# Ten of sixteen RWKV queries made beside the fronts and sent through DRAM, where four were kept on chip, and inversions that trace their products some rounds later

## The chip, the core and the metric

The kernel runs on one core of a Trainium2 chip. The core has five engines that run side by side, each through its own instructions in a fixed order: TensorE (PE) for matmuls, VectorE (DVE) and ScalarE (ACT) for elementwise work, GpSimd (POOL), and SyncE (SP), which here only issues DMA transfers; POOL issues some as well. An engine waits on semaphores for what another engine or a transfer has made. The metric is the device time of one execution in microseconds (us).

## The reference

One inference step of a two-layer encoder, D_MODEL = 2048, for 256 prompt tokens and 32 sample tokens (288 columns together). Layer 0 mixes with an mLSTM and an RG-LRU, layer 1 with RWKV-7 time mixing of 32 heads of 64; behind each mixer stands a squared-ReLU MLP. The change lies in layer 1:

```python
r = xr @ p['c_w_r'][li]
k = xk @ p['c_w_k'][li]
v = xv @ p['c_w_v'][li]
...
def step(S, inp):
    r_t, k_t, v_t, kk_t, a_t, w_t = inp
    sa = jnp.einsum('bhvk,bhk->bhv', S, -kk_t)
    S = S * w_t[:, :, None, :] + sa[..., None] * (kk_t * a_t)[:, :, None, :] + v_t[..., None] * k_t[:, :, None, :]
    return S, jnp.einsum('bhvk,bhk->bhv', S, r_t)
...
out = ((y + bonus) * g) @ p['c_w_o'][li]
```

`r` is the query that reads the state. The kernel works in chunks of 64 tokens, so for each head and chunk a triangular 64x64 matrix has to be inverted.

## The kernel before, in words

Heads are taken two at a time: 16 pairs of 128 rows. Dense products are made in three matmuls each (high and low part of the weights and of the activations), so the query of one pair is 16 tiles, 48 matmuls of 288 columns. Weights come in slabs of 8 tiles (512 KB, tile `raw`, three buffers); ACT makes the high part `whi` and DVE the low part `wlo`.

Two stages matter here.

**The fronts.** `run` advances generators by rounds, one step of each in a round, and a scheduler then orders the instructions. Three streams run: `front(p)` for each pair makes its decay and keys and stores them (`big`) and the matrix `nm` (`n`) in DRAM; `inverse16(q)` for each two pairs loads the 16x16 diagonal blocks (`nb`), inverts them on POOL in 15 steps of `tmp` and `tb`, and stores them (`t<-tb`); after some rounds (`for _ in range(5)`) `inverse(p, nm)` loads them as `tq`, and after some more (`range(3)`) traces the products on PE that make the inverse of 64x64, which is stored for later (`t<-tts`). The third stream makes `v` for pairs 2 to 15 (PE reads `hC`, `lC`), stored in DRAM, and then the queries of the first RPRE = 4 pairs in `r_proj` (PE reads `hD`, `lD`). These stay on chip in the dictionary RP. STEP and REST say after how many tiles a product of `r_proj` lets how many rounds pass.

**wkv.** `beside` advances `wkv(p)` of up to WIDTH = 4 pairs, a new one every GAP = 11 rounds, in the order in which it is written (no scheduler here). After each step of a pair it adds RATE divided by the number of pairs to an account, and for each SIZE = 4 in it advances the generator `feed` by four tiles. `feed` makes the remaining queries (`ps<-hD`, `ps<-lD`), then the first half of the output projection (`ps<-hB`, weights `in_wo`), which waits for the eighth pair's result. While RP holds RPC queries, `feed` yields and does nothing: the tiles of that turn are not made up for. `wkv(p)` takes its query out of RP in its fourth step; there DVE multiplies it into `ak` (`ak<-r,ak`) and POOL into `bk`. What `feed` has left after the last pair runs at the end.

A period of eleven rounds holds for one pair: loads on SP (`ak`, `bk`, `T`, `sv`, `v`), transposes (`pm<-cst,bk`, `pm<-cst,v`), products by chunk (`pm<-ak,bk`, `pm<-bm,T`), the chain of states through four prompt chunks and one sample chunk (`pm<-sv,ak`, `pm<-sv,tk`, `py`), the head norm with an inverse square root on DVE (`st<-st`), the gate (`ps<-hg`) and the result (`yc`, split into `hB`, `lB`).

Of the kernel before, what the change touches and what calls it, by code (L numbers as in the profile page):

```python
# [7 lines left out]
F32 = mybir.dt.float32  # L8
# [8 lines left out]
N = NP + NS  # L17
# [24 lines left out]
def stream_step(ctx: ExitStack, tc: tile.TileContext, I, O):  # L42
    nc = tc.nc
    V, A, G, PE, SP = nc.vector, nc.scalar, nc.gpsimd, nc.tensor, nc.sync

    def pool(name, bufs=1, side=None, **kw):
        st = ExitStack()
        if side is not None:
            kw['side'] = side
        p = st.enter_context(tc.tile_pool(name=name, bufs=bufs, reuse_waits="tile", **kw))  # L50
        return st, p
# [25 lines left out]
    def tt(out, a, b, op, eng=None):  # L77
        (eng or V).tensor_tensor(out=out, in0=a, in1=b, op=op)  # L78
# [21 lines left out]
    def copy(out, a):  # L100
        act(out, a, AF.Copy)

    def mm(out, lhsT, rhs, start=True, stop=True):
        PE.matmul(out, lhsT, rhs, start=start, stop=stop, skip_group_check=True)  # L104
# [106 lines left out]
    def dense_g(srcs, xs, m=128, step=4, rest=1):  # L211

        yield from hold()
        ps = psum.tile([128, 512], F32, name="ps", bufs=NPS)
        n = len(xs)
        for s, src in enumerate(srcs):
            kt = min(KS, n - s * KS)
            wh, wl = slab(src, kt, m)
            for k in range(kt):
                g = s * KS + k  # L220
                mm3(ps[:m, :N], (wh[:, k, :], wl[:, k, :]), xs[g], g == 0, g == n - 1)
                if g % step == step - 1:
                    for _ in range(rest):
                        yield
        free()
        return ps[:m, :N]
# [28 lines left out]
    def pm():  # L255
        return psum.tile([128, 512], F32, name="pm", tag="m", bufs=NPM)
# [545 lines left out]
    st_hid, hid = pool("hid", side="right")  # L802
# [185 lines left out]
    st_1, t1 = pool("t1")  # L988
# [4 lines left out]
    def scr(name, shape):  # L993
        return tc.dram_tile(shape, F32, name=name)
# [35 lines left out]

    RP = {}

    def r_proj(ps_):
        for p in ps_:
            while len(RP) == RPC:
                yield
            pr = yield from dense_g([I['wr'][p, s] for s in range(2)], xr, step=STEP, rest=REST)
            r = hid.tile([128, N], F32, name="r", tag="wa", bufs=4)
            copy(r, pr)
            RP[p] = r  # L1040
            yield

    NMB = 7
    GAPF = 6
    lastf = [-99]
    IE = G
    RPC, RPRE, GAP = 4, 4, 11
    WIDTH, RATE, SIZE, EXTRA = 4, 1.8, 4, 0.4
    NG = 1
    ended = set()  # L1050
    STEP, REST = 8, 6
    NM = {}
    done = set()
    def front(p):
# [64 lines left out]
    def flat(x):  # L1119
        return x.rearrange("p c t -> p (c t)")  # L1120

    def inverse16(q):

        while 2 * q + 1 not in NM:
            yield
        yield
        nb = t1.tile([80, 16, 16], F32, name="nb", bufs=1)
        G.dma_start(nb, bass.AP(tensor=SN[q].tensor, offset=SN[q].offset, ap=[[BS, 80], [C, 16], [1, 16]]))
        tb = t1.tile([80, 16, 16], F32, name="tb", bufs=2)
        SP.dma_start(tb, I['eye'])  # L1130
        for s in range(15):
            w, n = 15 - s, s + 1
            tmp = t1.tile([80, 64], F32, name="tmp", bufs=2)
            tv = tmp[:, :w * n].rearrange("p (a b) -> p a b", b=n)
            tt(tv, nb[:, s, s + 1:].unsqueeze(2).to_broadcast([80, w, n]),
               tb[:, s, :n].unsqueeze(1).to_broadcast([80, w, n]), OP.mult, eng=IE)
            tt(tb[:, s + 1:, :n], tb[:, s + 1:, :n], tv, OP.add, eng=IE)
            if s % 2:
                yield
        for i in range(2):  # L1140
            dst = bass.AP(tensor=S16[q].tensor, offset=S16[q].offset + i * (16 * 32 + 16),
                          ap=[[1024, 40], [32, 16], [1, 16]])
            G.dma_start(dst, tb[i:80:2])
        for _ in range(5):
            yield
        on = [inverse(2 * q, NM[2 * q]), inverse(2 * q + 1, NM[2 * q + 1])]
        while on:
            for g in list(on):
                try:
                    next(g)  # L1150
                except StopIteration:
                    on.remove(g)
            yield

    def inverse(p, nm):


        def f2(name):
            return t1.tile([128, NC, 32], F32, name=name, tag="f2", bufs=7)

        tq = f2("tq")
        G.dma_start(tq, S16[p // 2][p % 2].rearrange("c p t -> p c t"))

        def blocks(f):
            pz = pm()[:, :160].rearrange("p (c t) -> p c t", t=32)
            for c in range(NC):
                f(pz, c)
            return pz

        def quad(f):  # L1170
            def g(pz, c):
                for q in range(4):
                    r = slice(32 * q, 32 * q + 32)
                    l, x = f(r, 32 * (q % 2), c)
                    mm(pz[r, c, :], l, x)
            return blocks(g)

        for _ in range(3):
            yield
        xq = f2("xq")  # L1180
        V.transpose(flat(xq), flat(tq))
        pz = quad(lambda r, o, c: (nm[r, c, o:o + 32], tq[r, c, :]))
        yield
        zz = f2("zz")
        tt(zz, pz, mblk[:, None, :].to_broadcast([128, NC, 32]), OP.mult)
        yield
        pz = quad(lambda r, o, c: (xq[r, c, :], zz[r, c, :]))
        yield
        t32 = f2("t32")
        tt(t32, tq, pz, OP.add)  # L1190
        x32 = f2("x32")
        V.transpose(flat(x32), flat(t32))

        los = [slice(64 * h, 64 * h + 32) for h in range(2)]
        his = [slice(64 * h + 32, 64 * h + 64) for h in range(2)]

        def off(pz, c):
            for lo, hi in zip(los, his):
                mm(pz[hi, c, :], nm[lo, c, 32:64], t32[lo, c, :])

        yield
        pz = blocks(off)
        yield
        z2 = f2("z2")
        for hi in his:
            copy(z2[hi], pz[hi])

        def off2(pz, c):
            for hi in his:
                mm(pz[hi, c, :], x32[hi, c, :], z2[hi, c, :])  # L1210

        yield
        pz = blocks(off2)
        yield
        tt_ = tts[p % 2]
        for lo, hi in zip(los, his):
            copy(tt_[lo, :, 0], t32[lo])
            copy(tt_[hi, :, 1], t32[hi])
            copy(tt_[hi, :, 0], pz[hi])
        yield  # L1220
        SP.dma_start(ST[p], tt_)
        done.add(p)
# [63 lines left out]
    def ahead():  # L1286
        yield next(other)

    run(stream([front(p) for p in range(PAIRS)], 2), stream([inverse16(q) for q in range(PAIRS // 2)], 2),
        stream([v_proj(range(VPRE, PAIRS)), r_proj(range(RPRE)), ahead()], 1))  # L1290

    st_1.close()
# [7 lines left out]
    def f3(name, w=W, bufs=3):  # L1300
        return t2.tile([128, W], F32, name=name, bufs=bufs)[:, :w]
# [34 lines left out]
    def wkv(p):  # L1336
# [16 lines left out]
        pcs = bk[:, 2 * W + N:]  # L1353
        vf = f3("v", W, 4)
        DQ.dma_start(vf, SV[p])
        yield
        yield

        def tok(x, out):

            x = x.rearrange("p c t -> p (c t)")
            pz = pm()[:, :384].rearrange("p (a h t) -> p a h t", a=3, h=2)
            for j in range(3):
                w = 128 if j < 2 else 64
                PE.transpose(pz[:w, j].rearrange("p h t -> p (h t)"), x[:, 128 * j:128 * j + w], ident)  # L1365
            yield
            for i in range(2):
                for h in range(2):
                    copy(out(h)[:, i::2], pz[HH[i], :3 - i, h])
# [10 lines left out]

        bm = t2.tile([128, 2, NC, C], F32, name="bm", bufs=2)
        yield from tok(b_, lambda h: bm[HH[h], 0])
        while p not in RP:
            yield
        r = RP.pop(p)
        for h in range(2):
            R = flat(ak[HH[h], h, 1])[:, :N]
            tt(R, r[HH[h]], R, OP.mult)
# [120 lines left out]
    with tc.manual_schedule():  # L1509
        beside([wkv(p) for p in range(PAIRS)], WIDTH, GAP, other, RATE, SIZE)  # L1510
# [124 lines left out]
def _build(nc, arrays):  # L1635
    ins = {n: nc.dram_tensor(f"in_{n}", a.shape, F32, kind="ExternalInput").ap() for n, a in arrays.items()}
    outs = {n: nc.dram_tensor(f"out_{n}", s, F32, kind="ExternalOutput").ap() for n, s in _OUT.items()}
    with tile.TileContext(nc, schedule_with_timeline_sim=True) as tc:
        stream_step(tc, ins, outs)
# [13 lines left out]
```

## Time and profile before

| | us |
|---|---|
| median of three runs | 3341.88 (3338.5 to 3342.61) |
| the profiled execution | 3340.57 |
| its span, from first to last instruction | 3338.4 |
| PE busy | 3217.9 (96%) |
| DVE busy | 2120.1 (64%) |
| ACT busy | 1628.0 (49%) |
| POOL busy | 551.3 (17%) |

The profile is of one execution. Its page gives busy times by engine, the span in 40 slices, and the granted clock of PE (PEclk, 1.00 is full speed); views of the trace give the same for any stretch, the waits of an engine with what ended them, and the instructions in order of time. Times of a view count from the start of the span. Busy time of PE includes time in which its pipeline is only being filled; a share near 100% says that it waited for nothing, not that it worked at its peak. The page's line of PE by slices has nines nearly throughout, except in the slices of the fronts and some before them, in which also the clock falls; the fronts lie at about 1858 to 2100 us, wkv at about 2100 to 2432.

### The profile page before, as it was taken

The page shows a single profiled execution, that of the slowest core. Times are in us where ns is not written, and L with a number is a line of the kernel's source. Part 1 is how long each engine was busy: PE and PEld are TensorE (multiplying, and loading weights), DVE is VectorE, ACT ScalarE, POOL GpSimd, SP SyncE. Part 2 cuts the span into 40 slices and gives each one's busy share as a digit, 9 for nine tenths or more (in the row PEclk, how much of TensorE's full clock was granted, in tenths as well). Part 3 has the DMA queues.
Part 4 walks back from the last instruction along what each step waited for, and adds up shares of the span by engine and source line. Part 5 has one row for each costly group of instructions (what it writes and reads, how often), then busy time and mean ns, then how long its engine had stood idle before and what let it go on. Part 6 is the DMA issues. An engine that isn't in the chain of part 4 may idle for free.

```text
span 3338.4 us, 66879 instructions
## 1 busy us (share of the span) xinstructions
PE 3217.9 (96%) x26763; PEld 3120.9 (93%) x26763; DVE 2120.1 (64%) x3838; ACT 1628.0 (49%) x3070; POOL 551.3 (17%) x899
## 2 busy tenths in 40 slices
PE   9999999999999999999889888999989999999997
PEld 8999999999999999999878877788889999999997
DVE  6777777755655545456588664677777455454565
ACT  4444444444634435345465554676646344353443
POOL 0101111111000000001488256111240000000013
PEclk9999999999999999999999978999999999999998
DMA  6444444455554554555444765444454555555553
GB/s 209 149 154 156 151 156 147 146 180 180 164 167 165 165 165 165 164 165 160 162 125 138 235 201 162 149 137 136 152 171 161 167 165 165 164 164 165 165 164 123
DMA packets 195081, 540.60 MB, mean 162 GB/s; under 512 B 39179, under 2 KB 74251, under 8 KB 194771
## 3 DMA queue, kind: packets, MB, share of 16 engines
q1 hardware_dynamic: 190322, 526.95, 48.8%
q0 software_dynamic: 4448, 9.39, 1.2%
q8 instruction: 210, 3.44, 0.4%
q14 instruction: 101, 0.82, 0.1%
HBM read 500.81 MB, written 35.41 MB: 161 GB/s over the span
## 4 chain that ended last, share of the span: by engine, by line
PE 36%; POOL 4%; DVE 3%; DMA 3%; issue 2%; ACT 2%; SPq 0%; ACTq 0%; POOLq 0%; DVEq 0%
PE ps L104 32%; PE pm L104 3%; POOL tb L78 1%; POOL xx L78 1%; DVE wlo L78 1%; DVE x L78 1%; POOL tmp L78 1%; DMA t<-tb 1%; DMA nb<-n 1%; PE pm L1365 1%; PE py L104 0%; DMA tq<-t 0%; DMA v<-v 0%; ACT whi L98 0%; POOL xx L81 0%
## 5 line engine op out<-in xcount | busy, mean ns | idle before, releaser
L78 DVE TENSOR_TENSOR wlo<-raw,whi 128x1024 fp32r<-128x1024 f32 (+1 forms) x1018 | 1102.0, 1090 | 842.2 <-ACT whi L98 836.0
L98 ACT ACTIVATE whi<-raw 128x1024 fp32r<-128x1024 f32 (+1 forms) x1018 | 942.5, 936 | 1297.1 <-PE ps L104 1137.3
L104 PE MATMUL ps<-hB,whi 128*128 128x290 f32 (+1 forms) x3792 | 1133.9, 299 | 9.2 <-DVE x L78 2.8
L104 PE MATMUL ps<-hB,wlo 128*128 128x290 f32 (+1 forms) x3792 | 1131.3, 298 | 4.4 <-DVE wlo L78 4.4
L104 PE MATMUL ps<-lB,whi 128*128 128x290 f32 (+1 forms) x3792 | 1126.4, 297 | 4.9 <-DVE lB L78 4.9
L104 PEld LDWEIGHTS ps<-hB,whi 128*128 128x128 f32 x3792 | 718.8, 190 | 16.2 <-issue 5.1
L104 PEld LDWEIGHTS ps<-lB,whi 128*128 128x128 f32 x3792 | 719.9, 190 | 10.7 <-DVE lB L78 6.3
L104 PEld LDWEIGHTS ps<-hB,wlo 128*128 128x128 f32 x3792 | 717.3, 189 | 7.2 <-DVE wlo L78 6.0
L104 PE MATMUL ps<-hD,wlo 128*128 128x288 f32 (+1 forms) x1584 | 469.4, 297 | 6.6 <-DVE wlo L78 6.6
L104 PE MATMUL ps<-hD,whi 128*128 128x288 f32 (+1 forms) x1584 | 475.0, 300 | 0.3 <-ACT whi L98 0.3
L104 PE MATMUL ps<-lD,whi 128*128 128x288 f32 (+1 forms) x1584 | 468.9, 296 | 3.2 <-POOL lD L78 1.8
L104 PE MATMUL ps<-hC,whi 128*128 128x288 f32 (+1 forms) x1552 | 462.5, 298 | 5.4 <-ACT v L98 4.5
L104 PE MATMUL ps<-hC,wlo 128*128 128x288 f32 (+1 forms) x1552 | 460.2, 297 | 0.0
L104 PE MATMUL ps<-lC,whi 128*128 128x288 f32 (+1 forms) x1552 | 459.1, 296 | 0.0
L104 PEld LDWEIGHTS ps<-hD,wlo 128*128 128x128 f32 (+1 forms) x1584 | 300.3, 190 | 8.1 <-DVE wlo L78 7.9
L104 PEld LDWEIGHTS ps<-lD,whi 128*128 128x128 f32 (+1 forms) x1584 | 300.5, 190 | 4.1 <-POOL lD L78 2.0
L104 PEld LDWEIGHTS ps<-hD,whi 128*128 128x128 f32 (+1 forms) x1584 | 299.5, 189 | 4.5 <-issue 1.9
L104 PEld LDWEIGHTS ps<-hC,whi 128*128 128x128 f32 (+1 forms) x1552 | 293.5, 189 | 6.8 <-ACT v L98 5.6
L104 PEld LDWEIGHTS ps<-lC,whi 128*128 128x128 f32 (+1 forms) x1552 | 295.3, 190 | 0.3
L104 PEld LDWEIGHTS ps<-hC,wlo 128*128 128x128 f32 (+1 forms) x1552 | 294.4, 190 | 0.4
L78 POOL TENSOR_TENSOR acc<-x,x 128x288 f32<-128x288 f32 x8 | 8.6, 1079 | 1515.4 <-DVE x L78 1511.5
L78 DVE TENSOR_TENSOR x<-x,ps 128x288 f32<-128x288 f32 x96 | 43.6, 454 | 101.3 <-PE ps L104 100.6
(355 smaller groups left out, 3345.9 us busy)
## 6 DMA issues: line engine op xcount, KB each, us to landing
raw<-in_w SPq DMA_DIRECT2D x512, 512.0 KB, 3.4
raw<-in_win SPq DMA_DIRECT2D x160, 512.0 KB, 3.3
raw<-in_wout SPq DMA_DIRECT2D x64, 512.0 KB, 3.3
raw<-in_wk SPq DMA_DIRECT2D x32, 512.0 KB, 3.4
raw<-in_wv SPq DMA_DIRECT2D x32, 512.0 KB, 4.1
raw<-in_wr SPq DMA_DIRECT2D x32, 512.0 KB, 4.0
raw<-in_wo SPq DMA_DIRECT2D x32, 512.0 KB, 3.4
big<-big SPq DMA_DIRECT2D x16, 786.5 KB, 4.8
```

What stands on the lines that cost most here:

```text
L78: (eng or V).tensor_tensor(out=out, in0=a, in1=b, op=op)
L98: return A.activation(out, a, f, **kw)
L104: PE.matmul(out, lhsT, rhs, start=start, stop=stop, skip_group_check=True)
L1365: PE.transpose(pz[:w, j].rearrange("p h t -> p (h t)"), x[:, 128 * j:128 * j + w], ident)
```

## The change

`r_proj` now makes the queries of pairs 0 to 9 (RPRE = 10), each in a tile of its own pool, and stores it in DRAM (`SR[p]`) instead of keeping it; `wkv(p)` loads it into the tile that `feed` uses for its queries, as the last of its loads. `feed` has six queries left instead of twelve, and RP may hold two (RPC) instead of four. RATE goes from 1.8 to 1.3; STEP and REST from 8 and 6 to 4 and 2. The inversions let eight rounds pass instead of five before `inverse`, and six instead of three before its products.

```diff
--- before.py
+++ after.py
@@ -1030,25 +1030,26 @@
 
     RP = {}
 
+    SR = {}
+
     def r_proj(ps_):
         for p in ps_:
-            while len(RP) == RPC:
-                yield
             pr = yield from dense_g([I['wr'][p, s] for s in range(2)], xr, step=STEP, rest=REST)
-            r = hid.tile([128, N], F32, name="r", tag="wa", bufs=4)
+            r = t1.tile([128, N], F32, name="r", bufs=2)
             copy(r, pr)
-            RP[p] = r
+            SR[p] = scr(f"r{p}", [128, N])
+            SP.dma_start(SR[p], r)
             yield
 
     NMB = 7
     GAPF = 6
     lastf = [-99]
     IE = G
-    RPC, RPRE, GAP = 4, 4, 11
-    WIDTH, RATE, SIZE, EXTRA = 4, 1.8, 4, 0.4
+    RPC, RPRE, GAP = 2, 10, 11
+    WIDTH, RATE, SIZE, EXTRA = 4, 1.3, 4, 0.4
     NG = 1
     ended = set()
-    STEP, REST = 8, 6
+    STEP, REST = 4, 2
     NM = {}
     done = set()
     def front(p):
@@ -1141,7 +1142,7 @@
             dst = bass.AP(tensor=S16[q].tensor, offset=S16[q].offset + i * (16 * 32 + 16),
                           ap=[[1024, 40], [32, 16], [1, 16]])
             G.dma_start(dst, tb[i:80:2])
-        for _ in range(5):
+        for _ in range(8):
             yield
         on = [inverse(2 * q, NM[2 * q]), inverse(2 * q + 1, NM[2 * q + 1])]
         while on:
@@ -1175,7 +1176,7 @@
                     mm(pz[r, c, :], l, x)
             return blocks(g)
 
-        for _ in range(3):
+        for _ in range(6):
             yield
         xq = f2("xq")
         V.transpose(flat(xq), flat(tq))
@@ -1353,6 +1354,9 @@
         pcs = bk[:, 2 * W + N:]
         vf = f3("v", W, 4)
         DQ.dma_start(vf, SV[p])
+        if p in SR:
+            rl = hid.tile([128, N], F32, name="r", tag="wa", bufs=4)
+            SP.dma_start(rl, SR[p])
         yield
         yield
 
@@ -1380,9 +1384,9 @@
 
         bm = t2.tile([128, 2, NC, C], F32, name="bm", bufs=2)
         yield from tok(b_, lambda h: bm[HH[h], 0])
-        while p not in RP:
-            yield
-        r = RP.pop(p)
+        while p not in RP and p not in SR:
+            yield
+        r = RP.pop(p) if p not in SR else rl
         for h in range(2):
             R = flat(ak[HH[h], h, 1])[:, :N]
             tt(R, r[HH[h]], R, OP.mult)
```

The dense matmuls are the same in number and stand elsewhere in PE's order. From the first product of the last inversion (`pm<-tq,nm`) to the first instruction of wkv there are 36 before and 200 now, of which 143 stand behind the inversion's last product. Inside wkv, up to the last pair's gate, there are 960 before (576 `hD` and `lD`, 384 `hB` and `lB` of `wo`) and 504 now; 168 of `wo` follow behind. Three places show it.

PE, in wkv, before: the end of a pair's step and the start of a block of twelve dense matmuls (`ps<-hD`, `ps<-lD`), of which half are shown.

```order
L104 MATMUL py<-tk_24775,sv 64x64 x2
L1365 MATMUL pm<-cst,v 128x128 x2
L1365 MATMUL pm<-cst,v 64x128
L104 MATMUL pm<-sv,ak 64x64 x2
L104 MATMUL py<-ak,sv 64x64 x2
L104 MATMUL pm<-ak,bk 64x64 x6
L104 MATMUL ps<-hD,whi 128x288
L104 MATMUL ps<-lD,whi 128x288
L104 MATMUL ps<-hD,wlo 128x288
L104 MATMUL ps<-hD,whi 128x288
L104 MATMUL ps<-lD,whi 128x288
L104 MATMUL ps<-hD,wlo 128x288
```

The same place of a pair's program in the changed order, here between the third and the tenth pair:

```order
L104 MATMUL py<-tk_25173,sv 64x64 x2
L1369 MATMUL pm<-cst,v 128x128 x2
L1369 MATMUL pm<-cst,v 64x128
L104 MATMUL pm<-sv,ak 64x64 x2
L104 MATMUL py<-ak,sv 64x64 x2
L104 MATMUL pm<-ak,bk 64x64 x10
L104 MATMUL pm<-sv,tk_25174 64x64 x2
L104 MATMUL py<-tk_25174,sv 64x64 x2
L1369 MATMUL pm<-cst,bk 128x128 x2
L1369 MATMUL pm<-cst,bk 64x128
```

Before, a block follows the products `pm<-ak,bk` of two chunks; now the next products follow directly. PE's changed order has no `hD` or `lD` between pairs over a stretch of eight pairs: the gates of pairs 0 to 7 (`ps<-hg`) all stand inside it, and the next block comes when pair 10 has taken its query.

POOL, between the second and the third inversion of 16x16, before: the store of the inverses, the load of `tq`, then the load of the next `nb`.

```order
L78 TENSOR_TENSOR tb<-tb,tmp 80x15
L1143 DMA t_9401<-tb 40x16x16 x2
L1162 DMA tq<-t_9401 128x5x32 x2
L1128 DMA nb<-n_20819 80x16x16
L78 TENSOR_TENSOR tmp<-nb,tb 80x15
L78 TENSOR_TENSOR tb<-tb,tmp 80x15
L78 TENSOR_TENSOR tmp<-nb,tb 80x28
```

And now:

```order
L78 TENSOR_TENSOR tb<-tb,tmp 80x15
L1129 DMA nb<-n_20819 80x16x16
L1144 DMA t_9401<-tb 40x16x16 x2
L78 TENSOR_TENSOR tmp<-nb,tb 80x15
L78 TENSOR_TENSOR tb<-tb,tmp 80x15
L78 TENSOR_TENSOR tmp<-nb,tb 80x28
L78 TENSOR_TENSOR tb<-tb,tmp 80x14x2
L78 TENSOR_TENSOR tmp<-nb,tb 80x39
L78 TENSOR_TENSOR tb<-tb,tmp 80x13x3
L1163 DMA tq<-t_9401 128x5x32 x2
L78 TENSOR_TENSOR tmp<-nb,tb 80x48
```

Here the next `nb` is asked for first, and `tq` is loaded in the middle of the next inversion. At other places it is the reverse: of the seven passages from one inversion to the next, three run as store, `tq`, `nb`, two as store, `nb`, `tq`, and two as `nb`, store and `tq` later, as many of each in the one order as in the other.

SP, from the fronts to wkv, before: `T` and `sv` are what wkv(0) loads on this queue (`ak`, `bk` and `v` of pair 0 go through POOL's).

```order
L127 DMA raw<-in_wr 128x1024 x3
L1234 DMA raw<-in_wr 128x1024 x2
L1221 DMA t_20813<-tts_20825 128x320
L1221 DMA t_20814<-tts_20827 128x320
L1221 DMA t_20815<-tts_20825 128x320
L1221 DMA t_20816<-tts_20827 128x320
L1346 DMA T<-t_20801 128x320
L1349 DMA sv<-in_S 64x64 x2
L1234 DMA raw<-in_wr 128x1024 x2
L190 DMA raw_24930<-in_l2g 128x256
```

And now (`r_24276` to `r_25147` are the queries in DRAM):

```order
L1041 DMA r_25017<-r 128x288
L1235 DMA raw<-in_wr 128x1024
L1041 DMA r_25082<-r 128x288
L1041 DMA r_25147<-r 128x288
L1347 DMA T<-t_20801 128x320
L1350 DMA sv<-in_S 64x64 x2
L1359 DMA r<-r_24276 128x288
L1235 DMA raw<-in_wr 128x1024 x2
L190 DMA raw_25330<-in_l2g 128x256
L1343 DMA ak<-big_20786 64x640 x2
```

The loads of wkv(0) stand behind the stores of the inversions before, and behind the store of the tenth query now; the load of the first query is the last of them.

## Rows read from the trace of the kernel before

**Rows 1.** The page, part 1: each engine's busy us, share, instructions.

```profile
PE 3217.9 (96%) x26763; PEld 3120.9 (93%) x26763; DVE 2120.1 (64%) x3838; ACT 1628.0 (49%) x3070; POOL 551.3 (17%) x899
```

**Rows 2.** Windows of three stretches: length; busy us by engine; PEclk; DMA share; GB/s.

```profile
1858.20:2099.50 241.30, 199.67 (x3192) 185.16 (x3190) 144.76 (x385) 122.27 (x288) 133.72 (x295) 0.87 0.65 192
2099.50:2432.40 332.90, 323.12 (x3690) 275.19 (x3690) 250.81 (x811) 218.11 (x688) 51.68 (x107) 1.00 0.48 149
2600.00:2650.00 50.00, 50.00 (x380) 50.00 (x379) 24.18 (x27) 17.43 (x20) 0.00 (x0) 1.00 0.51 165
```

**Rows 3.** Waits of PE, 1858 to 2100: us in all, times, longest.

```profile
PE pm L104 <- DMA tq<-t: 33.6, 9, 8.5
```

**Rows 4.** POOL by lines, 1884 to 2088: busy, mean ns | idle before, releasers.

```profile
L78 POOL TENSOR_TENSOR tmp<-nb,tb 80x15 f32<-80x15 f32 (+7 forms) x120 | 44.5, 370 | 31.7 <-DMA nb<-n 23.0
L1162 POOL DMA_DIRECT2D tq<-t x16 | 14.2, 890 | 25.5 <-DMA t<-tb 10.7 <-PE ps L104 5.3 <-DVE kkn L84 4.4
L1128 POOL DMA_DIRECT2D nb<-n x8 | 7.7, 966 | 55.1 <-DMA raw<-in_l2wa 48.7 <-DMA v<-v 3.8 <-DMA n<-nm 2.2
```

**Rows 5.** PE's timeline, one period of wkv: start us, us, what.

```profile
2204.45 0.38 PE L104 MATMUL ps<-hg,whi 128*128 128x288 f32 x1
...
2207.15 0.41 PE L104 MATMUL ps<-hD,whi 128*128 128x288 f32 x1
...
2208.93 0.27 PE L104 MATMUL pm<-ak,bk 64*64 64x64 f32 x2
...
2222.74 0.38 PE L104 MATMUL ps<-hg,whi 128*128 128x288 f32 x1
```

**Rows 6.** Timeline of POOL and of DVE about 2054.5.

```profile
2054.40 0.26 POOL L78 TENSOR_TENSOR tmp<-nb,tb 80x39 f32<-80x39 f32 x1
2054.73 1.14 POOL L78 TENSOR_TENSOR tb<-tb,tmp 80x39 f32<-80x39 f32 x1
...
2054.53 1.23 DVE L78 TENSOR_TENSOR wlo<-raw,whi 128x1024 fp32r<-128x1024 f32 x1 [3.68 <-ACT whi L98]
```

**Rows 7.** PE's timeline, last inversion and first instruction of wkv.

```profile
2089.02 1.61 PE L104 MATMUL pm<-tq,nm 32*32 32x32 f32 x80 [3.23 <-DMA tq<-t]
...
2100.29 0.55 PE L1365 MATMUL pm<-cst,bk 128*128 128x128 f32 x3
```

**Rows 8.** SP's timeline, issue of wkv(0)'s load of T.

```profile
2101.80 0.44 SPq L1346 DMA_DIRECT2D T<-t  x1
```

**Rows 9.** DMA issues, 1850 to 2440: count, KB each, median us to landing.

```profile
k<-kd SPq DMA_DIRECT2D x16, 144.0 KB, 3.9
```

**Rows 10.** DVE by lines, four periods of wkv.

```profile
L84 DVE SCALAR_TENSOR_TENSOR st<-st 96x6 f32<-96x6 f32 x24 | 3.9, 162 | 0.8
...
L78 DVE TENSOR_TENSOR ak<-r,ak 64x288 f32<-64x288 f32 x8 | 3.6, 448 | 0.1
L81 DVE TENSOR_SCALAR st<-st 96x6 int32<-96x6 int32 x4 | 2.3, 568 | 0.1
...
L84 DVE SCALAR_TENSOR_TENSOR yc<-yc,vec,v 128x288 f32<-128x288 f32 x4 | 2.1, 519 | 0.1
...
L78 DVE TENSOR_TENSOR st<-st 96x6 f32<-96x6 f32 x12 | 1.9, 162 | 0.4
```

**Rows 11.** Windows, the same four periods, all instructions.

```profile
2188.88:2262.26 73.38, 73.29 (x867) 62.12 (x864) 58.32 (x193) 51.38 (x165) 8.92 (x20) 1.00 0.43 133
```

**Rows 12.** Windows, the same, instructions on raw weights: DVE, ACT.

```profile
2188.88:2262.26 73.38, 13.85 (x36) 13.15 (x36) 1.00 0.43 133
```

**Rows 13.** Waits of PE, 2425 to 2500.

```profile
PE pm L1015 <- ACT e L98: 3.8, 1, 3.8
```

**Rows 14.** Windows of two stretches of small matmuls.

```profile
2128.81:2133.55 4.74, 3.89 (x76) 3.01 (x75) 2.71 (x11) 3.49 (x13) 0.58 (x1) 1.00 0.34 111
1921.10:1928.80 7.70, 7.20 (x187) 6.15 (x187) 5.88 (x20) 5.98 (x19) 6.17 (x14) 0.50 0.62 200
```

**Rows 15.** PE's timeline, 80 small matmuls at full clock.

```profile
1945.60 0.91 PE L104 MATMUL pm<-zz,xq 32*32 32x32 f32 x80
```

## The prediction

> **What bounds the kernel now.** I read the page first: TensorE (PE) is busy for 96% of the span, VectorE (DVE) for 64, ScalarE (ACT) for 49 [rows 1]. So the time is PE's work plus what PE waits, plus what it loses at half clock. The change leaves PE's work as it is: the same sixteen queries of 48 dense matmuls are made. It only moves some of them from the last RWKV stage into the one before. What counts is therefore what each stage lets PE lose, and I read the two stages by windows next.
>
> The stage of the fronts and inversions lasts 241.3 us; PE is busy for 199.7 of them, and its granted clock averages 0.87. The stage of the sixteen pairs (wkv) lasts 332.9 us, with PE busy for 323.1 at a clock of 1.00 [rows 2]. So the first has room for more matmuls and the second has nearly none. The waits of PE in the first stage say why: 33.6 us in 9 waits are for the load of `tq`, the 16x16 inverses that GpSimd (POOL) made [rows 3]. POOL's groups of instructions show the chain behind it: besides the arithmetic there is idle time in front of the `tq` issues (25.5 us) and of the products (31.7 us, most of it for `nb`) [rows 4]. POOL sets the pace there, PE fills in.
>
> **The change part by part.** All sums stand against the profiled execution, 3340.57 us (span 3338.4); the median shown, 3341.88, is 1.3 above it.
>
> *Dense matmuls, price of one.* 380 of them take 50.0 us where nothing else runs [rows 2]: 0.1316 us. Between wkv's small matmuls they stand in blocks of 12 (four tiles); such a block runs from 2207.15 to 2208.93, 1.78 us [rows 5], where 12 x 0.1316 would be 1.58. The block pays 0.2 us for the change of form.
>
> *Front stage.* Six queries more are made there: 6 x 48 x 0.1316 = 37.9 us of PE. POOL's chain has the same links in both orders: of its seven passages from one inversion to the next three run "store, load tq, load nb" one after the other, two have nb between, two have nb first. So the 3 + 3 more rounds don't shorten it; they reorder it. What can go is POOL's own wait for the fronts before issuing `nb`: 2.2 + 3.8 = 6.0 us [rows 4]. What comes: while DVE splits a whole weight slab (`wlo`, 1.23 us), a POOL operation takes 1.14 us where its neighbour takes 0.26 [rows 6]. Twelve slabs are added, about six of them ahead of POOL's last inversion; POOL is busy about half of the stage (133.7 of 241.3 us [rows 2]), so half of them meet one of its operations: 6 x 0.5 x 0.88 = 2.6 us. The Trainium skill ("SBUF — State Buffer", Terms) says that these two engines arbitrate for one port pair, held for a full instruction, and that the loser blocks; the row agrees. By the page the price is up to a whole split for each of the six, 6 x 1.23 = 7.4 us instead of 2.6. By the rows POOL's last `tq` comes at -6 + 2.6 = -3.4 us. Behind it PE must still run, in the written order, 200 dense matmuls instead of 36 before the first wkv instruction; before, that way took from 2089.02 to 2100.29 [rows 7]. The 164 more are 21.6 us. The front stage ends at -3.4 + 21.6 = **+18.2 us**, so about half of the 37.9 is hidden in PE's waits. From both sides: nothing hidden is +37.9; if the idle in front of `tq` that waits for the store (10.7 us) went as well, +8.
>
> *Queries through DRAM.* Ten stores on SP's queue wait for their copy, as the stores of `v` did, and the slab loads behind them lead by two slabs; ten loads lie far ahead of their use. I take these at nothing, except the first load. In SP's order the loads of wkv(0) (T, sv, r) stand behind the store of the last query. After PE's last dense matmul come the copy (about as long as DVE's product `ak`, 0.45 [rows 10]), then four issues on SP (the store, T and two of sv) at T's 0.44 [rows 8], then a load of 144 KB that lands after 3.9, as `k` does [rows 9], then two products `ak`: 0.45 + 1.76 + 3.9 + 0.9 = 7.0. PE has 2.8 us to do meanwhile (two groups of transposes of about 0.5, one block of 1.78). So PE waits **+4.2 us**, bounds 0 and 7.0.
>
> *Pairs without filling.* This is the term that decides. The generator `feed` makes two queries (r10, r11), and then may hold no third until wkv(10) takes one. So from the third pair to the tenth, eight pair periods, no dense block stands between wkv's matmuls. Now a period is 18.29 us (2204.45 to 2222.74) with four blocks [rows 5]; without them PE has 18.29 - 4 x 1.78 = 11.2. But then the other engines come level. In four periods (73.4 us) DVE was busy 58.3 and ACT 51.4, of which splits of weights 13.9 and 13.2 [rows 11, 12]; what stays is 11.1 and 9.6 us a pair. No less than 11.2, then, and more, since DVE's work is lumpy: in one of a pair's eleven rounds stands rsqrt, ten small `st` operations of together (3.9 + 2.3 + 1.9)/4 = 2.0 us; in another two products `ak` and two operations on `yc`, 2 x 0.45 + 2 x 0.52 = 1.9 us [rows 10]. A round of PE is 11.2/11 = 1.0 us, so each lump keeps PE waiting for about 1 us. I take 11.2 + 2.0 = 13.2. Bounds: 11.2, and 18.3 (nothing gained by taking blocks out). Eight pairs: 8 x (13.2 - 18.29) = **-40.7 us** (from -57 to 0).
>
> *Other blocks.* By PE's order 960 dense matmuls (80 blocks) stood in wkv's stage, all between pairs' work; now 504 (42 blocks) do, and 168 follow the last pair. In the eight pairs above 32 were; the rest goes from 48 to 42: -6 x 1.78 = **-10.7**. The 168 behind cost 168 x 0.1316 = **+22.1**.
>
> *Tail.* At the end of wkv PE waits 3.8 us for the last pair's `e` [rows 13]; more dense work now stands there: **-2** (0 to -3.8).
>
> Sum: 18.2 + 4.2 - 40.7 - 10.7 + 22.1 - 2 = -8.9. From 3340.57 that is 3331.7, and with the 1.3 up to the median 3333.0: **3333 us**, 0.27% faster. The change is nearly an exchange: about 20 us less loss in the fronts, about as much more between pairs; what tips it is 38 blocks fewer that pay 0.2 us each.
>
> **The rivals.**
> 1. *Half clock between the pairs (slower).* Small matmuls alone may not keep the clock. Speaking for it: in 1921.1 to 1928.8 PE was busy 7.20 of 7.70 us with nearly only small matmuls, after a long wait, and stayed at 0.50, the lower level, 1.2 GHz [rows 14]. Against: in 2128.81 to 2133.55 only small ones ran, with 0.85 us idle, and the clock stayed at 1.00 (2.4 GHz) [rows 14]. Once low, it would remain so until dense blocks return at pair 10. 80 small matmuls took 0.91 us at full and 1.61 at half clock [rows 7, 15], 1.77 times; with 1.7 for the mixture a pair takes 11.2 x 1.7 = 19.0, so 8 x (19.0 - 13.2) = +46: 3379. It decides as soon as one wait early among the eight pairs pulls the clock down. The Trainium skill ("TensorE: Matmul & The Clock Gate", Part 1: The HAM clock gate) says that activity releases the throttle and an idle stretch brings it back; by it the short waits between pairs leave the clock alone and this rival falls away, but the first of the two rows, busy and still low, doesn't agree with it.
> 2. *The pairs hardly shorten.* Should the lumps of three engines meet, a period of 16 us: 8 x 2.8 = +22, 3355; at 18.3, 3374.
> 3. *The fronts hide nothing:* +37.9 instead of 18.2, so 3353. For it: PE's order ends with 143 dense matmuls that nothing overlaps. Against: PE waits 33.6 us for `tq` alone.
> 4. *No change:* a period of 14.2 instead of 13.2 gives 3341. Little speaks against it.
> 5. *More gained:* a period of 12.2 and fronts of +10: -8 - 8 below the forecast, 3317.
>
> **How the numbers follow.** A measurement of this kernel tells 0.2%, 6.7 us, from no change. Chances: my forecast and rival 5, below 3335.2: 0.48 (rival 5 alone 0.12). Rival 4 with the near part of the others, 3335.2 to 3348.6: 0.23. Above: rival 1 0.13, rival 2 0.10, rival 3 0.06, together 0.29. The forecast's own range, from its bounds of the period (12.2 to 14.2) and of the fronts, is 3317 to 3345. For eight in ten I go down to 3312 and up to 3366, which takes in rivals 2 and 3 but not the full price of rival 1.
>
> **What would show it.** Right: PE busy about 85% with gaps of about 1 us, behind DVE, in eight equal periods of about 13 us with no `hD` matmul in them; the clock at 1.00 there; wkv's first matmul about 18 us later than 2100.3, then a wait of some 4 us for `r`; fewer and shorter waits for `tq`; 56 tiles of `wo` behind the last pair. Wrong: PEclk of 5 in the slices of the unfilled pairs (rival 1), periods over 15 us (rival 2), a first wkv matmul after 2130 (rival 3).

## The result, and the profile after

The changed kernel takes 3364.68 us (median of 4 runs, 3361.46 to 3368.0) against 3342.24 for the kernel before (4 runs): a ratio of 1.007, 95% interval 1.0057 to 1.0083. It is slower by 22 us; forecast was 9 faster. The profiled execution has a span of 3364.5 us against 3338.4, so 26.1 us are to be found.

The page, part 1, of the changed kernel (each engine's busy us, share, instructions). It answers [rows 1]: PE has the same 26763 instructions and the same 96%, so what grew is what PE loses.

```profile
PE 3219.2 (96%) x26763; PEld 3123.6 (93%) x26763; DVE 2115.3 (63%) x3802; ACT 1626.8 (48%) x3034; POOL 554.2 (16%) x899
```

I cut both traces at the same four events: first matmul of the fronts, first wkv matmul, end of the last gate matmul of the last pair, first matmul of the statistics behind the output projection `wo`. The windows view of the three stretches (columns as in [rows 2]), first of the kernel before, then of the changed one:

```profile
1858.19:2100.29 242.10, 200.47 (x3232) 185.88 (x3230) 144.77 (x385) 122.90 (x290) 133.72 (x295) 0.87 0.64 192
2100.29:2432.58 332.29, 322.51 (x3655) 274.67 (x3650) 250.81 (x811) 217.48 (x686) 51.68 (x107) 1.00 0.48 150
2432.58:2443.38 10.80, 10.80 (x81) 10.80 (x79) 4.53 (x6) 3.56 (x6) 0.80 (x1) 0.96 0.42 125
```

```profile
1860.84:2131.64 270.80, 233.82 (x3521) 219.65 (x3520) 156.93 (x395) 139.03 (x310) 132.58 (x292) 0.92 0.67 200
2131.64:2415.00 283.36, 256.84 (x3194) 211.55 (x3192) 218.32 (x729) 188.25 (x604) 45.07 (x95) 0.99 0.42 130
2415.00:2468.53 53.53, 39.90 (x244) 38.65 (x245) 19.62 (x43) 13.60 (x31) 8.89 (x16) 0.87 0.58 180
```

Subtract line by line: fronts +28.7 (forecast +18.2), the pairs -48.9 (forecast 4.2 - 40.7 - 10.7 - 2 = -49.2), the rest of `wo` behind the last pair +42.7 (forecast +22.1). The remaining +3.6 are 2.65 us that the fronts start later and 1 us behind these stretches. So the stage of the pairs, which I said decides, came out within half a microsecond in its sum (in part by luck, as the account of the forecast below shows); the fronts and the rest of `wo` did not.

**The pairs.** From 2165.6 to 2275.9 no dense block stands between the pairs' matmuls, eight pairs long, and seven periods from one `ps<-hg` to the next lie in it whole, all within 0.02 us of each other. The changed kernel's timeline of PE, one of them (start us, length us):

```profile
2178.90 0.38 PE L104 MATMUL ps<-hg,whi 128*128 128x288 f32 x1
...
2183.00 0.34 PE L104 MATMUL pm<-sv,tk 128*64 128x64 f32 x4 [1.09 <-ACT sv L98]
...
2190.48 0.34 PE L104 MATMUL pm<-sv,ak 128*64 128x64 f32 x4 [0.43 <-DVE sv L84]
...
2191.84 0.34 PE L104 MATMUL pm<-sv,tk 128*64 128x64 f32 x4 [0.51 <-ACT sv L98]
...
2192.76 0.38 PE L104 MATMUL ps<-hg,whi 128*128 128x288 f32 x1
```

A period is 13.86 us (forecast 13.2; 18.29 in [rows 5]). The seven as one window:

```profile
2178.90:2275.92 97.02, 82.27 (x1179) 62.76 (x1177) 81.48 (x281) 68.72 (x224) 15.99 (x35) 1.00 0.40 118
```

PE is busy 85% at a clock of 1.00, its upper level. Rival 1 is refuted: small matmuls with 2.1 us of short waits per period keep the clock for 97 us. PE's waits in the same stretch:

```profile
PE pm L104 <- ACT sv L98: 11.2, 14, 1.1
PE pm L104 <- DVE sv L84: 3.0, 7, 0.4
```

They are for `sv`, the evacuated state, on ACT more than DVE; I had put them behind DVE's `st` and `ak`.

**The first load of r.** SP's timeline and DVE's waits of the changed kernel: `r` is issued behind the two last stores, `T` and two `sv`, as counted in [rows 8], and DVE and PE wait for it.

```profile
2126.76 5.89 SPq L1041 DMA_DIRECT2D r<-r  x2
2132.70 0.42 SPq L1347 DMA_DIRECT2D T<-t  x1
2133.18 1.16 SPq L1350 DMA_DIRECT2D sv<-in_S  x2
2134.44 0.53 SPq L1359 DMA_DIRECT2D r<-r  x1
...
DVE ak L78 <- DMA r<-r: 9.4, 1, 9.4
...
2137.46 0.30 PE L104 MATMUL pm<-ak,bk 64*64 64x64 f32 x2 [3.40 <-issue]
2138.38 0.89 PE L104 MATMUL pm<-ak,bk 64*64 64x64 f32 x16 [0.62 <-DVE ak L78]
```

PE waits 3.40 + 0.62 = 4.0 us (forecast 4.2). For the first of the two waits the view names no releaser ("issue"); DVE's line names the load, and DVE's first product `ak` starts at 2136.91, 0.55 us ahead of PE's. The sum was right, its parts only together: the load landed 2.5 us after its issue at 2134.44 (3.9 counted), while the issues and the two products took longer than counted.

**Behind the last pair.** PE's waits in that stretch, the timelines of POOL and of DVE:

```profile
PE ps L104 <- DVE xres L84: 9.3, 4, 3.3
PE ps L104 <- DVE x L78: 2.7, 1, 2.7
...
2433.43 0.45 DVE L84 SCALAR_TENSOR_TENSOR xres<-xres,ps 128x288 f32<-128x288 f32 x1 [4.26 <-DMA xres<-xd]
2434.19 0.54 POOL L1282 DMA_DIRECT2D xp<-xres  x1 [3.75 <-DVE xres L84]
2434.73 0.54 POOL L1278 DMA_DIRECT2D xres<-xd  x1
2438.60 0.45 DVE L84 SCALAR_TENSOR_TENSOR xres<-xres,ps 128x288 f32<-128x288 f32 x1 [3.37 <-DMA xres<-xd]
2439.35 0.54 POOL L1282 DMA_DIRECT2D xp<-xres  x1 [4.08 <-DVE xres L84]
2439.88 0.54 POOL L1278 DMA_DIRECT2D xres<-xd  x1
2443.51 0.45 DVE L84 SCALAR_TENSOR_TENSOR xres<-xres,ps 128x288 f32<-128x288 f32 x1 [3.11 <-DMA xres<-xd]
```

Read it as a ring: DVE adds a tile of `wo`'s product to `x`; POOL, which waited for that, stores it (`xp`) and only then issues the load of the next `x`; DVE waits for the load. One turn is 5.2 us (2433.43 to 2438.60), while 24 dense matmuls of a row tile want 24 x 0.1316 = 3.2. In the kernel before, turns of 4.8 to 5.6 us lie beside the last pairs' work, and PE has no wait for `xres` from 2360 to 2445.

**The fronts.** PE's waits and POOL's group of `tq`, answering [rows 3] and [rows 4], and the answer to [rows 7]:

```profile
PE pm L104 <- DMA tq<-t: 25.7, 8, 5.1
...
L1163 POOL DMA_DIRECT2D tq<-t x16 | 14.2, 890 | 32.7 <-PE pm L104 12.4 <-PE ps L104 6.8 <-DVE kkn L84 5.8
...
2099.67 1.06 PE L104 MATMUL pm<-tq,nm 32*32 32x32 f32 x80
...
2131.64 0.49 PE L1369 MATMUL pm<-cst,bk 128*128 128x128 f32 x3
```

The waits for `tq` fell by 8 us only. The last `tq` matmul stands 238.8 us after the stage's start (230.8 before): +8.0 where I had -3.4. From there to wkv 32.0 us (11.3 before): +20.7 where I had +21.6. By the windows, 288 more dense matmuls raised PE's busy time by 33.4 us (4.5 less than the 37.9 counted, as the clock rose from 0.87 to 0.92) and took 4.7 us of PE's idle time away (41.6 to 37.0). Hidden: 9.2 of 37.9 us.

The first part of the forecast for this stage, POOL's chain, can be read from POOL's other groups: `tb` of the kernel before (its `tmp`, `tq` and `nb` are [rows 4]), then three of the changed kernel.

```profile
L78 POOL TENSOR_TENSOR tb<-tb,tmp 80x15 f32<-80x15 f32 (+7 forms) x120 | 47.5, 396 | 9.4
```

```profile
L78 POOL TENSOR_TENSOR tb<-tb,tmp 80x15 f32<-80x15 f32 (+7 forms) x120 | 47.6, 396 | 9.4
L78 POOL TENSOR_TENSOR tmp<-nb,tb 80x15 f32<-80x15 f32 (+7 forms) x120 | 44.1, 368 | 31.4 <-DMA nb<-n 22.7
L1129 POOL DMA_DIRECT2D nb<-n x8 | 7.7, 966 | 54.0 <-DMA raw<-in_l2wa 48.4 <-DMA t<-tts 5.2 <-issue 0.4
```

The idle time before `nb` fell by 1.1 us (55.1 to 54.0), not by 6.0; the products took 91.7 us in all (92.0 before), not 2.6 more; and the idle time before `tq`, which the forecast left as it was, grew by 7.2 (25.5 to 32.7).

### The profile page after: what moved, and what is told of

Same layout as the page of the kernel before. It is cut to its first block, busy times and chain, and to the rows that moved or that the text cites. A ratio compares the mean times of both kernels' runs of the same rounds, so it can differ in the third digit from the quotient of the medians.

```text
span 3364.5 us, 66882 instructions
## 1 busy us (share of the span) xinstructions
PE 3219.2 (96%) x26763; PEld 3123.6 (93%) x26763; DVE 2115.3 (63%) x3802; ACT 1626.8 (48%) x3034; POOL 554.2 (16%) x899
## 5 line engine op out<-in xcount | busy, mean ns | idle before, releaser
L104 PE MATMUL ps<-hB,whi 128*128 128x290 f32 (+1 forms) x3792 | 1136.1, 300 | 22.1 <-DVE xres L84 9.3
L104 PEld LDWEIGHTS ps<-hB,whi 128*128 128x128 f32 x3792 | 721.8, 190 | 28.8 <-issue 13.2
```

## The experiments

All of them are timed against the kernel before, five rounds each, in three groups; the kernel before had medians of 3341.27, 3339.98 and 3338.55 in them, so the ratios are compared. A ratio can differ from that of the medians by up to 0.07%, some 2 us. Stage lengths come from one profiled execution of each, cut as above. The fronts differ by some microseconds between executions: 270.8, 268.2, 265.0, 275.1 and 268.2 us with ten queries and the same edits in that stage (the changed kernel, e3, e4, e5, e11); with four queries 242.1 (the kernel before), and 239.9 and 240.1 (e1 and e8, with the later rounds).

### The later rounds alone (e1_inv_only)

```diff
 (kernel before)
-        for _ in range(5):
+        for _ in range(8):
...
-        for _ in range(3):
+        for _ in range(6):
```

> The kernel before with only the inversions' 3 + 3 more rounds. Theory A (the later rounds lengthen GpSimd's chain: in the changed kernel its last load of tq ends 209 us after its first load of nb, 203 before): the front stage is 5 to 9 us longer, 3347 to 3351 in all. Theory B (the rounds are harmless, the 143 dense matmuls that stand alone behind the last inversion are what the fronts lose): no change, 3336 to 3344, with fewer waits for tq.

Measured 3341.39, ratio 0.9999 (0.999 to 1.0007). The later rounds cost nothing by themselves, as theory B had it; the fewer waits for `tq` that it expected did not come (33.2 us in 9, against 33.6 in 9).

### The ten queries with the earlier rounds (e2_inv_back)

```diff
 (changed kernel)
-        for _ in range(8):
+        for _ in range(5):
...
-        for _ in range(6):
+        for _ in range(3):
```

> The changed kernel with the inversions' rounds put back to 5 and 3. Theory A: 5 to 9 us faster than the changed kernel's 3364.7, 3356 to 3360. Theory B: the same or slower than it, 3362 to 3372, since still more dense matmuls (277 in PE's order) then stand alone behind the last inversion.

Measured 3367.87, ratio 1.0086 (1.0072 to 1.01): theory A is refuted. The fronts of this kernel last 281.5 us, 39.4 over the kernel before. Its last `tq` product stands 231.8 us after the stage's start (230.8 before), and the way from there to wkv takes 49.7 us instead of 11.3: all of the 288 added matmuls stand behind that product (324 dense matmuls in the trace instead of 36), and nothing of them is hidden. (The profiled execution took 7 us more than the median, so the size is known to some microseconds only.) With the later rounds the fronts average 269.4 us, so part of the queries is hidden there; how much of that the rounds give isn't settled, as the intervals of the two ratios overlap.

### The load of x off POOL's queue (e3_x_sp)

```diff
 (changed kernel)
-            G.dma_start(x, xd[n])
+            SP.dma_start(x, xd[n])
```

> The changed kernel with the load of x for the first half of wo issued on SP instead of GpSimd's queue, where it stands behind the store of the row tile before. Theory: the 168 dense matmuls behind the last pair go at 5 us for 24 because product, sum, store and next load follow each other; without that they go at 3.2 to 3.5 us, and the kernel is 13 to 18 us faster than the changed one, 3347 to 3352. Rival (the weights' slabs or half clock hold them up): within 3 us of 3364.7.

Measured 3351.02, ratio 1.0032 (1.002 to 1.0043): 13 us back from one word. The window behind the last pair and PE's waits in it:

```profile
2412.64:2451.62 38.98, 35.02 (x245) 34.21 (x246) 19.81 (x42) 14.42 (x33) 5.97 (x9) 0.96 0.74 248
...
PE ps L104 <- DVE xres L84: 2.7, 2, 2.0
PE ps L104 <- DVE x L78: 0.8, 1, 0.8
```

The same 245 matmuls take 38.98 us in place of 53.53; the idle time falls from 13.6 to 4.0 us, the busy time from 39.9 to 35.0 with the clock from 0.87 to 0.96. The ring was the cause, and the clock its second price. At 0.1316 each the 245 would be 32.2.

### Six queries ahead in place of two (e4_rpc6)

```diff
 (changed kernel; the "wa" tiles get 8 buffers in place of 4)
-    RPC, RPRE, GAP = 2, 10, 11
+    RPC, RPRE, GAP = 6, 10, 11
```

> The changed kernel where feed may hold six queries (eight buffers), so that it fills pairs 2 to 6 too and nearly nothing is left behind the last pair. Theory: some four pairs of 13.9 us go back to 18.3, +18, and the 42.7 us more behind the last gate go, 3338 to 3343. Rival (what stands behind the last pair costs its matmuls only, 22 us, and the fronts are the loss): 3358 to 3362.

Measured 3336.87, ratio 0.9994 (0.9985 to 1.0003), a little better than expected: 25 us under the changed kernel by the ratios, 28 by the medians. Windows of fronts, pairs and rest:

```profile
1859.80:2124.76 264.96, 231.41 (x3521) 217.63 (x3519) 156.29 (x395) 139.00 (x310) 134.09 (x292) 0.94 0.67 205
2124.76:2426.49 301.73, 279.64 (x3363) 234.21 (x3361) 235.08 (x764) 198.15 (x629) 52.49 (x109) 0.99 0.45 145
2426.49:2436.35 9.86, 9.86 (x75) 9.86 (x75) 5.38 (x8) 2.90 (x6) 2.19 (x2) 1.00 0.56 170
```

Dense work goes back among the pairs for 18.4 us and saves 43.7 behind them. That is the exchange the change had made the wrong way round: with a feed that may hold two queries, blocks of `wo` were left over while pairs ran unfilled.

### The first pair's r over POOL's queue (e5_first_r)

```diff
 (e4_rpc6; DQ is POOL's queue for the first pair, SP's for the others)
-            SP.dma_start(rl, SR[p])
+            DQ.dma_start(rl, SR[p])
```

> The kernel with six queries fed to the pairs (e4_rpc6), with one more edit: the load of a pair's r goes out on POOL's queue instead of SP's. Theory (the wait of about 4 us before the second block of the wkv stage is the first pair's load, held up in SP's queue): the wait goes, 4 us less than e4_rpc6, 3331 to 3334. Rival (something else is waited for at the same place, or POOL's own chain pays): within 1.5 us of e4_rpc6, 3335.5 to 3338.5, or above it.

Measured 3329.82, ratio 0.997 (0.9958 to 0.9981). From the first wkv matmul to the first pair's gate, e4_rpc6 and then this kernel:

```profile
2124.76:2174.72 49.96, 44.24 (x541) 37.96 (x540) 30.09 (x91) 31.26 (x102) 6.00 (x13) 0.97 0.52 174
```

```profile
2134.22:2178.23 44.01, 42.33 (x541) 36.31 (x540) 28.90 (x89) 31.43 (x102) 4.79 (x10) 1.00 0.59 193
...
2099.43 0.54 POOL L1360 DMA_DIRECT2D r<-r  x1
```

Six us shorter: 4.0 of idle time and 1.9 of busy time, since the wait had cost the clock as well (0.97 against 1.00). POOL issues the load at 2099.43, 35 us ahead of the stage; on SP it stood behind the stores of the queries. (The profiled execution had long fronts, 275.1 us, and took 7 us more than the median.)

### v earlier in PE's order (e6_v_step4)

```diff
 (e4_rpc6; v_proj gets a parameter step, 2 elsewhere)
-        stream([v_proj(range(VPRE, PAIRS)), r_proj(range(RPRE)), ahead()], 1))
+        stream([v_proj(range(VPRE, PAIRS), 4), r_proj(range(RPRE)), ahead()], 1))
```

> e4_rpc6 with one number changed: the projections of v beside the fronts let the round go on after 4 tiles instead of 2, so PE's order carries its dense matmuls earlier in the fronts and about 55 fewer of them stand behind the last inversion. Theory (what is hidden is decided by the written order: the queries were written behind the point at which POOL's chain ends): the fronts shrink by 10 to 20 us against e4_rpc6, 3317 to 3328. Rival (POOL's chain sets the end of the fronts, wherever PE's matmuls stand, and its inversions now come later too): within 4 us of e4_rpc6, 3333 to 3341.

Measured 3330.02, ratio 0.9965 (0.9951 to 0.9978): 7 us under e4_rpc6 by the medians, 10 by the ratios, about the theory's least (10); the rival's 4 are passed. The fronts take 259.0 us, 10.4 under the average of the five kernels with ten queries; the waits for `tq` fall to 7.5 us in 4, and a wait for `big` on DVE (11.6 in 3) takes part of their place. The edit did more to the order than expected: no dense matmul stands behind the last `tq` product (200 in e4_rpc6), and from there to wkv it is 7.0 us (32.2). But that product now stands 252.0 us after the stage's start, 21.2 more than in the kernel before: about half of the 42.6 us (324 matmuls) that have moved ahead of it. So order decides, but no more than a part comes back: the extra matmuls also stand ahead of PE's own links in the chain.

### Seven queries in the fronts (e7_seven), and seven with the two last edits (e10_seven_both)

```diff
 (e4_rpc6; e10 is the same edit on e9 below)
-    RPC, RPRE, GAP = 6, 10, 11
-    WIDTH, RATE, SIZE, EXTRA = 4, 1.3, 4, 0.4
+    RPC, RPRE, GAP = 6, 7, 11
+    WIDTH, RATE, SIZE, EXTRA = 4, 1.55, 4, 0.4
```

> e4_rpc6 with seven queries beside the fronts instead of ten, and nine fed to the pairs at a rate of 1.55. Theory (by the order, the queries of the fronts past the seventh stand behind the last inversion, bare): the fronts shrink by about 3 x 48 x 0.1316 = 19 us, of which the pairs take back 8 to 14 through being filled longer: 3323 to 3335. Rival (a query costs the same in the fronts as beside the pairs): 3335 to 3339, as e4_rpc6.

> e9_both with seven queries beside the fronts and nine fed to the pairs (rate 1.55). Theory (a query costs the same at either place once both are filled without holes): within 4 of e9_both, 3319 to 3328. Rival (with v earlier ten queries hide better in the fronts, and seven leave PE waiting there again): 3328 to 3334.

e7: 3340.0, ratio 0.9995 (0.9986 to 1.0004). The fronts fall to 246.3 us, 18.7 less than e4_rpc6, which is the full price of three queries (18.9): the eighth to tenth had been bare. (Both are single executions; e7's took 6 us less than its median.) But the pairs take 19.9 more (321.66), so the gain is nil, and the rival holds. e10: 3339.62, ratio 1.0002 (0.9993 to 1.0011), 15 us over e9 and beyond even its rival. With v earlier there is no dense work left when POOL makes its last inverses; a window behind the last dense matmul of the fronts, and PE's waits in it:

```profile
2079.28:2112.82 33.54, 12.92 (x483) 10.83 (x483) 5.47 (x17) 10.47 (x33) 19.55 (x51) 0.54 0.26 74
...
PE pm L104 <- DMA tq<-t: 17.7, 3, 12.4
```

For 33.5 us PE is busy 12.9, at a clock of 0.54, nearly all of it the lower level. The pairs take 19.9 us more than in e9, as in e7, but the fronts fall by 7.8 only (253.2 against 261.0), where e7 gave 18.7. With v earlier, then, the last three queries were of use as cover, which the rival had said.

### Only the count undone (e8_four)

```diff
 (changed kernel; the "wa" tiles get 8 buffers in place of 4)
-    RPC, RPRE, GAP = 2, 10, 11
-    WIDTH, RATE, SIZE, EXTRA = 4, 1.3, 4, 0.4
+    RPC, RPRE, GAP = 4, 4, 11
+    WIDTH, RATE, SIZE, EXTRA = 4, 1.8, 4, 0.4
```

> The changed kernel with the count alone undone: four queries beside the fronts and up to four ahead in the feed, rate and steps as before, while the route through DRAM and the later rounds of the inversions stay. Theory (only the count and the place of the matmuls cost; the route through DRAM costs no more than the wait for the first r): 3337 to 3346, as the kernel before. Rival (the copies, stores and loads themselves cost, by SP's queue or by DVE): 3348 or more.

STEP and REST stay as changed, 4 and 2, though the text above has the steps as before. Measured 3348.58, ratio 1.002 (1.0012 to 1.0029): about 7 us over the kernel before by the ratio, 8.6 by the medians. The number is the rival's; the place, as the windows show, is the theory's, and only the price of the first r was too low. The fronts are the same (240.1). The first two gate periods together, with the same 192 dense matmuls in both, kernel before and this one, with DVE's wait:

```profile
2100.29:2167.88 67.59, 64.36 (x774) 54.45 (x768) 44.73 (x140) 46.20 (x149) 6.96 (x15) 1.00 0.54 166
```

```profile
2101.24:2175.73 74.49, 67.63 (x770) 57.51 (x768) 44.84 (x140) 44.91 (x145) 8.21 (x18) 0.95 0.48 158
...
DVE ak L78 <- DMA r<-r: 8.6, 1, 8.6
```

6.9 us, half idle (3.6), half busy at a lower clock (3.3). From the second pair's gate on the periods agree with the kernel before within 0.06 us. So the way through DRAM costs the first pair 6 to 7 us, with four queries as with ten, and the later pairs nothing.

### The edits together (e9_both, e11_after_two, e12_after_three)

```diff
 (e9: e4_rpc6 with the edits of e5 and e6; e11: changed kernel with those of e3 and e5;
  e12: e11 with that of e6)
```

> e4_rpc6 with the two edits of e5_first_r and e6_v_step4 together: the first pair's r comes over POOL's queue, and the projections of v beside the fronts stand earlier in PE's order. Theory (two places, two costs, that add up; each edit alone gave about 7): 3320 to 3326. Rival (the one gain takes the other's place, since both lie around the first pair of the wkv stage): 3328 to 3332.

> The changed kernel with two of its three named losses taken away and everything else as changed: the loads of x behind the last pair go out on SP's queue (e3_x_sp), and the first pair's r on POOL's (e5_first_r). Theory (the losses are separate and add: 13.7 for the first, 7 for the second): 3342 to 3347. Rival (the load of r costs the first pair only what it waits for otherwise): 3349 to 3353, as e3_x_sp.

> e11_after_two with the third loss attacked as well: the projections of v beside the fronts stand earlier in PE's order (e6_v_step4), so fewer dense matmuls are left behind the last inversion. Theory (the loss in the fronts is one of written order): 7 to 10 less than e11_after_two, 3333 to 3339, so the changed kernel's schedule beats the kernel before once its three side costs are off. Rival (POOL's chain sets the fronts' end): within 3 of e11_after_two.

e11: 3342.53, ratio 1.001 (1.0001 to 1.0019), and e12: 3335.69, ratio 0.9985 (0.9976 to 0.9993), both as the theories had it (e12 seven under e11). So the three edits together take 29 us off the changed kernel by the medians (3364.68 to 3335.69), and it then lies a little under the kernel before. e9: 3324.57, ratio 0.9951 (0.9938 to 0.9963), the fastest here, 14 us under the kernel before by the medians, 16 by the ratio. Its three stretches:

```profile
1857.99:2118.98 260.99, 229.83 (x3514) 217.12 (x3512) 156.95 (x394) 138.46 (x309) 136.70 (x293) 0.92 0.69 207
2118.98:2416.78 297.80, 279.57 (x3363) 234.27 (x3361) 235.29 (x764) 198.89 (x630) 52.71 (x109) 0.99 0.46 147
2416.78:2426.63 9.85, 9.85 (x75) 9.85 (x76) 5.39 (x8) 2.90 (x6) 2.19 (x2) 1.00 0.55 177
```

Against the kernel before: fronts +18.9, pairs -34.5, rest -1.0. The fronts cost here what I had forecast for the change, +18.2; it took the earlier v to get there.

## Why the prediction was wrong

By the profiles the forecast was -8.9 us and the change cost 26.1. Of the 35.0 between them 20.6 lie behind the last pair, 10.5 in the fronts, 0.3 in the pairs and 3.6 outside these stretches.

- *Pairs without filling*, -40.7: the mechanism was right, the size a little off: 8 x (13.86 - 18.29) = -35.4, nearer to the 14.2 of rival 4 than to my 13.2. Rival 1 (half clock) is refuted by a clock of 1.00 over 97 us, rival 2 by the period. The Trainium skill ("TensorE: Matmul & The Clock Gate", Part 1: The HAM clock gate) has activity release the throttle and idle bring it back; these pairs agree with it. The 7.7 us busy at the lower level in [rows 14] don't, and no run settles why.
- *Dense matmuls behind the last pair*, +22.1: the step that failed most, +42.7. I priced 168 matmuls at the rate of a stretch where nothing else limits them [rows 2], and did not ask what else each row tile of `wo` needs. POOL's queue holds the store of one tile ahead of the load for the next, 5.2 us a turn. The excess of 20.6 is 13.6 of idle time and the rest mostly clock (0.87); e3_x_sp shows it by moving the load alone. The Trainium skill ("DMA: Bandwidth & Descriptors", Anatomy of one DMA — SWDGE (gpsimd) path) says that a wait on a semaphore is spent on the issuing sequencer before dispatch; the trace agrees: POOL's store at 2434.19 stood waiting 3.75 us for DVE's sum, and the load was issued 0.54 us behind it.
- *Front stage*, +18.2: failed, +28.7. The sub-step that failed is the head: POOL's last `tq` and PE's last inversion were to come 3.4 us sooner and came 8.0 later; the tail (164 more matmuls, 21.6) measured 20.7. Neither term of the head came: -6.0 before `nb` was -1.1, +2.6 in the products was -0.3. What came, +7.2 before `tq`, was not in the sum. I treated PE's waits for `tq` as room for the queries. The matmuls fill them only where the written order has them just there, and they put off the chain where they stand ahead of its links. e2 (all 288 behind the last `tq` product, 39.4 of 37.9), e6 (7 to 10 us from the order of v alone) and e7 (the last three queries at full price) show it. In e4_rpc6, with the same order, the fronts came to 265.0, so of the 10.5 missed some 6 lie within what executions differ by; the five of this order average 269.4, which is +28.7 over the 240.7 of the three with four queries. Why POOL waited longer before `tq` (32.7 against 25.5) isn't settled: neither edit alone moves the last `tq` product (231.3 us after the stage's start in e1, 231.8 in e2, 232.7 to 239.7 in the five with both); the releasers named are PE's, but at the last one the landing of POOL's own store explains the wait as well.
- *First load of r*, +4.2: 4.0 of wait. Not in the sum was the clock behind it: e5_first_r gives 6.0 for the whole, e8_four 6.9.
- *Other blocks and tail*, -12.7: what is left of the stage's -48.9 is -48.9 + 35.4 - 6.0 = -19.5, 7 more than I had. So the -49.2 agrees with the measured sum because errors of +5.3, +1.8 and -6.8 cancel, which is luck; which part of the -19.5 is blocks and which tail was not told apart.
- The mark I had set against myself, a first wkv matmul after 2130, was met (2131.64), if narrowly: in three of the four other executions with this order it comes at 2124.8 to 2128.8. Rival 3 named the fronts, but neither it (3353) nor any rival had the wait behind the last pair, 20.6 of the 35.0 us of the miss. The larger error is an instruction count at its best rate, in a place where that rate had not been seen; the smaller one is a wait taken for room.

## What to carry to other kernels

Work that is moved out from behind a cover takes along its loads, stores and queue order: look at the period of the whole ring (load, compute, store) before pricing the matmuls at their own rate, and don't put a store that waits ahead of the next load on one queue. A wait of an engine is room for other work only if that work stands at that point of its order; count what stands behind the last link of the chain, and what is left to stand beside it. Keep fillers for all of the stretch that needs them: in the changed kernel (wkv unfilled, `wo` left over) the pairs and the rest shrank by only 6.2 us together though 37.9 us of matmuls had left them, and in e10 (nothing left beside the last inverses) the fronts gave back 7.8 us for 18.9 taken out.

## What the runs showed of the hardware that was not expected

Short waits add up at half clock: a wait of 4.0 us for `r` cost 1.9 more in busy time, and the 13.6 us behind the last pair went with about 8 (39.9 us busy at a clock of 0.87 for 244 matmuls that would take 32.1). Yet 97 us of small matmuls, busy 85% with waits of 1.1 us at most, ran at 1.00 throughout. A PE that is busy 12.9 of 33.5 us with small matmuls ran at 0.54.
